# A hybrid attention layer on one core: attention phases, output weight splits and transposes moved, last block stored in three pieces

## The chip, the cores and the metric

One core of a Trainium2 chip runs the whole program. The time is the device time of one execution in microseconds (us), as the median of several executions; lower is better. Engines are named as the profile names them: PE (TensorE, matrix products), PEld (its weight loads), DVE (VectorE), ACT (ScalarE), POOL (GpSimd), SP (SyncE, which issues most transfers). Each engine runs its own instructions strictly in the order of the program and waits for the others by semaphores.

## The reference

The input x is 512 rows of 1024 numbers, float32. One layer is computed and a final normalisation follows:

```python
h = rmsnorm(x, norm_g)
p = h @ w_in                 # split into 14 column groups
y_gla  = rmsnorm(gated_linear_attention(gq, gk, gv, glog)) * silu(ggate)      # 4 heads, 384 columns
y_dsa  = dsa_mixer(dq, dk, dv, q_idx, k_idx, w_idx, rel_bias) * silu(dgate)   # 6 heads, 384 columns
y_pool = (windowed means of pu, minus pu) @ pool_w * pool_scale * silu(pgate) # 256 columns
x = x + concat(y_gla, y_dsa, y_pool) @ w_out
out = rmsnorm(x) * final_norm_g
```

dsa_mixer is causal softmax attention in which each row attends to the 128 visible keys with the highest indexer score (exactly the top 128), with a relative position bias.

## The kernel before, in words

**Tiles.** The 512 rows are 4 blocks of 128 (i or t = 0 to 3). Matrix products are made float32-exact out of three products of "high" and "low" parts: a tile is rounded to its high part by ACT (`hi_of`, L96), the rest becomes the low part on DVE (`lo_of`, L99), and PE computes high by high, low by high and high by low.

**First stage: input projections.** w_in comes in chunks of columns. A chunk's two halves (512 input rows each) are loaded by SP (`load_next`, L888), split by `half`, and multiplied by `proj_n` (one block of rows per step, L187) or `proj_t` (transposed, 128 columns per step, L199). A step of `proj_t` is 2 x 12 products of 512 columns into one PSUM bank. The order of the chunks that matter here is n4, dg, pg, c2, c1, pu, c0; c2, c1 and c0 hold the queries and keys of head pairs g = 2, 1, 0, pu and pg are the pooling branch, dg the attention gate.

**What sets the order.** The table `after` (L637 to L678) is written by hand: its key (chunk, step, "mid") names what is issued between the two halves of a projection step, (chunk, step) what is issued after the step, and "end" what is issued after its result has been taken out of PSUM. Everything hung in there is issued in that order on every engine that it uses. The top-k selection (`topk`, DVE, L458 and L459) fills the first stage in small portions.

**Linear attention (GLA).** For each block t: `gla_scores`, `gla_out` (PE L527, L531), `gla_norm`, `gla_gated` (DVE L564 writes gg), and `gla_turn`: PE transposes gg into the bank tpg (L571), ACT makes yGh, DVE yGl.

**Attention phases.** For block i and head pair g, named as letter, block, pair ("q02" is att_q(0, 2)): l lays the bias and mask into L on POOL (L689 to L696); q makes the scores on PE (L708), adds and takes the minimum on DVE (L710), and the exponential on ACT (L712); n takes the reciprocal of the sums on DVE (L719) and scales on POOL (L721); t transposes on PE (L730) and copies, the first head by ACT, the second by DVE (L732); v multiplies with the values (L741), DVE gates (yt, L744), ACT makes yDh; y makes yDl on DVE. The queries and keys of a pair are moved to the partitions where the scores need them by transfers that SP issues, QQ (L376) for the queries, KK and KL (L382) for the keys.

**Output weights.** w_out comes in four chunks wo0 to wo3. `out_high(n, h)` (ACT, tile oh) and `out_low(n, h)` (DVE, tile ol) split quarter h of chunk n, two instructions of 128 x 512 each. The first pieces of output weights take the tiles with the tags wh and wl, of which there are four each (bufs=4); the chunks before them in these four are pu half 0, pu half 1, c0 half 0 and c0 half 1, so out_high(0, 0) takes the tile of wh_pu0 and out_low(0, 0) that of wl_pu0.

**Second stage, `finish` (L815 on).** `out_part(t, a, e, kinds)` (PE L772) adds the products of block t for columns a to e of the output for G (GLA, 9 products), P (pooling, 6) and D (attention, 9); between these calls stand the remaining phases of pairs 1 and 0, the pooling products (`pool_mix`, PE L595, DVE L596), yPl (`pool_low`) and the splits. `residual` adds x, `out_norm` and `out_close` normalise and store. `out_last` (L793) does so for the last block, whose second half of columns comes in two pieces, 512 to 768 and 768 to 1024, so that only the last 256 columns stand behind the last matrix product:

```python
E = T + 256                                  # T = 512, D = 1024
out_part(t, E, D, "GPD", first=True, last=True)
```

Of the kernel before, what the change touches and what calls it, by code (L numbers as in the profile page):

```python
# [13 lines left out]
AF = mybir.ActivationFunctionType  # L14
ALU = mybir.AluOpType
# [3 lines left out]
T = 512  # L19
# [50 lines left out]
def hybrid_layer(  # L70
# [547 lines left out]
    def phase(n):  # L618
# [31 lines left out]
        ("dg", 0): [partial(gla_norm, 1), partial(gla_turn, 0), *halves("pg1"), partial(topk, 1, 1)],  # L650
        ("dg", 1, "mid"): [partial(gla_out, 2), partial(gla_scores, 3), partial(gla_gated, 1)],
        ("dg", 1): [partial(gla_norm, 2), partial(gla_turn, 1), *halves("c20", "c21"), partial(topk, 1, 3)],
        ("pg", 0, "mid"): [partial(gla_out, 3), partial(gla_gated, 2), partial(topk, 1, 2, 3)],
        ("pg", 0): [partial(gla_norm, 3), partial(gla_turn, 2), *halves("c10"), partial(topk, 1, 3)],
        ("pg", 1, "mid"): [partial(gla_gated, 3), partial(topk, 1, 2, 3)],
# [8 lines left out]
        ("c1", 0, "end"): [*halves("c00"), partial(topk, 1, 2)],  # L664
        ("c1", 1, "mid"): [partial(topk, 1, 2, 3)],
        ("c1", 1): [lambda: nc.gpsimd.memset(up[:, :, 0:16], 0.0), *att("l02", "l12"), partial(topk, 1, 3)],
        ("c1", 1, "end"): [lambda: load_next(), *halves("c01"), partial(topk, 16, 2, 3), *att("q02")],
        ("pu", 0, "mid"): att("n02", "q12"),
        ("pu", 0): att("t02", "n12", "l22"),
        ("pu", 1, "mid"): att("v02", "t12", "l32", "q22"),  # L670
        ("pu", 1): [*att("n22", "y02", "v12"), lambda: out_high(0, 0), lambda: pool_branch(0)],
        ("c0", 0, "mid"): [lambda: out_low(0, 0), *att("t22", "q32", "y12")],
        ("c0", 0): att("n32", "l01"),
        ("c0", 0, "end"): [lambda: out_high(1, 0), lambda: load_next(), *att("v22"), lambda: pool_branch(1)],
        ("c0", 1, "mid"): [lambda: out_low(1, 0), *att("t32", "q01", "l11", "y22")],
        ("c0", 1): att("n01"),
        ("c0", 1, "end"): [*att("v32", "q11", "l21"), lambda: out_high(0, 1)],
# [115 lines left out]
    def out_last(t):  # L793
        ts_ = slice(t * P, (t + 1) * P)
        E = T + 256
# [14 lines left out]
        nc.scalar.activation(xf[:, 0:T], xf[:, 0:T], AF.Copy, scale=fs[:, 4:5])  # L810
        nc.scalar.dma_start(o2[ts_, 0:T], xf[:, 0:T])
        nc.vector.tensor_scalar(xf[:, T:D], xf[:, T:D], fs[:, 4:5], None, op0=ALU.mult)
        nc.sync.dma_start(o2[ts_, T:D], xf[:, T:D])

    def finish():  # L815
# [7 lines left out]
        do("n11", "t01", "q21", "l00", "y32")  # L823
        out_high(1, 1)
        out_part(1, 0, T, "G", first=True)
        do("n21", "v01", "t11")
        out_low(1, 1)
        do("q00", "l31")
# [5 lines left out]
        pool_mix()  # L834
        out_part(2, 0, T, "G", first=True)
        do("n00", "v11", "t21", "y01")
        pool_low()
        do("q31", "l10")
        out_part(0, 0, T, "P")
        out_low(2, 0)  # L840
        do("n31", "v21", "t00", "q10", "l20", "y11")
        out_high(3, 0)
        out_part(1, 0, T, "P")
        do("n10", "v00", "t31", "q20", "l30", "y21")
        out_low(3, 0)
        out_high(2, 1)
        do("y00")
        out_part(2, 0, T, "P")
        out_part(0, 0, T, "D", last=True)
        do("n20", "v31", "t10", "q30")  # L850
        out_low(2, 1)
        out_high(3, 1)
        residual(0, 0, T, 0)
        out_low(3, 1)
# [25 lines left out]
        out_part(3, T, T + 256, "GPD", first=True, last=True)  # L880
# [7 lines left out]
    def load_next():  # L888
        n = len(chunks)
        if n < len(plan):  # L890
            chunks.append(load_chunk(*plan[n][:2]))
# [11 lines left out]
    def out_high(n, h):  # L903
        part, j = divmod(n, 2)
        cs = slice(256 * j, 256 * j + 256)
        for q in (2 * h, 2 * h + 1):
            if j == 0:
                WO[part].append(out_tiles(part, q))
            hi_of(WO[part][q][0][:, :, cs], chunks[n_in + n].raw[q // 2][:, 2 * (q % 2):2 * (q % 2) + 2, 0:256])
# [216 lines left out]
```

## Time and profile before

| what | value |
|---|---|
| median of 3 executions | 262.05 us (261.85 to 262.07) |
| profiled execution | 262.02 us, span in the profile 260.2 us |
| granted clock over it | 0.994 |
| PE busy | 245.0 us, 94% |
| DVE busy | 197.4 us, 76% |
| ACT, POOL busy | 119.6 us and 103.3 us |

The span runs from the first to the last instruction that the profile shows; 1.8 us lie around it. Times of the trace count from the start of the span. "Busy" of PE counts matrix products that overlap one another in the pipeline, so the time that one product really takes is read from start to start, not from its own length.

### The profile page before, as it was taken

What the parts mean: (1) busy time and instruction counts of PE and PEld (TensorE: products, weight loads), DVE (VectorE), ACT (ScalarE), POOL (GpSimd) and SP (SyncE); (2) the same over time, 40 slices, a digit from 0 to 9 for tenths busy, and PEclk for the clock granted to TensorE, in tenths of its full rate; (3) what the DMA queues carried; (4) which work ended last, traced back from release to release, by engine and by line L of the source; (5) the groups of instructions that cost most, each with busy time, mean ns of one, the idle gap of its engine ahead of it and who ended that gap; (6) DMA issues with size and microseconds to landing.
All of it is one profiled execution on the core that took longest, in us unless ns stands there. A gap on an engine that the chain in (4) does not pass through costs nothing.

```text
span 260.2 us, 4199 instructions
## 1 busy us (share of the span) xinstructions
PE 245.0 (94%) x1498; PEld 203.8 (78%) x1498; DVE 197.4 (76%) x442; ACT 119.6 (46%) x251; POOL 103.3 (40%) x109
## 2 busy tenths in 40 slices
PE   8999999999999999899999989998989978999990
PEld 4778889999999998688888867776756755788890
DVE  3999388899999999998999853599875877345322
ACT  5965186884836722225323353434465745222111
POOL 1645356354058630418534063618456562000011
PEclk9999999999999999999999999999999999999997
DMA  6994413225202150222314867605486000025012
GB/s 229 393 410 174 128 46 97 79 78 214 81 1 89 74 165 0 81 82 81 90 74 115 195 136 174 273 0 131 141 217 239 4 0 0 3 98 215 35 58 81
DMA packets 11780, 31.09 MB, mean 119 GB/s; under 512 B 1600, under 2 KB 1600, under 8 KB 11760
## 3 DMA queue, kind: packets, MB, share of 16 engines
q1 hardware_dynamic: 11328, 30.05, 36.2%
q10 hardware_dynamic: 432, 0.79, 0.9%
q8 instruction: 12, 0.20, 0.3%
q14 instruction: 8, 0.07, 0.1%
HBM read 23.91 MB, written 2.10 MB: 100 GB/s over the span
## 4 chain that ended last, share of the span: by engine, by line
PE 47%; DVE 36%; issue 6%; ACT 4%; DMA 3%; POOL 2%; SPq 1%; POOLq 0%; ACTq 0%; DVEq 0%
PE op L772 11%; DVE scs L459 8%; DVE m L458 6%; PE pf L973 5%; DVE ol L99 3%; PE pt_c L210 2%; PE pt_c L208 2%; PE pt_c L209 2%; DVE pm L583 2%; PE ov L741 2%; DMA wk<-in_w_in 2%; PE tpp L730 2%; ACT L L712 2%; DVE wl_n L99 2%; DVE wlk L99 2%
## 5 line engine op out<-in xcount | busy, mean ns | idle before, releaser
L721 POOL TENSOR_SCALAR L<-L,ast 128x128 f32<-128x128 f32 (+3 forms) x24 | 14.8, 630 | 34.1 <-DVE ast L719 34.1
L458 DVE MAX8 m<-scs 128x8 f32<-128x256 f32 (+2 forms) x48 | 26.5, 552 | 0.1
L459 DVE MATCH_REPLACE8 scs<-m,scs 128x256 f32<-128x256 f32 (+2 forms) x48 | 26.1, 543 | 0.0
L196 PE MATMUL pn_n<-wh_n,hTh 128*128 128x270 f32 (+1 forms) x128 | 21.6, 291 | 0.0
L196 PE MATMUL pn_n<-wl_n,hTh 128*128 128x270 f32 (+1 forms) x128 | 21.1, 287 | 0.0
L196 PE MATMUL pn_n<-wh_n,hTl 128*128 128x270 f32 (+1 forms) x128 | 21.0, 286 | 0.0
L712 ACT ACTIVATE L<-L,ast 128x128 f32<-128x128 f32 (+3 forms) x24 | 13.3, 557 | 16.0 <-DVE ast L710 15.1
L208 PE MATMUL pt_c<-hTh,wh_c 128*128 128x512 f32 x48 | 19.3, 402 | 0.0
L210 PE MATMUL pt_c<-hTh,wl_c 128*128 128x512 f32 x48 | 19.0, 395 | 0.0
L209 PE MATMUL pt_c<-hTl,wh_c 128*128 128x512 f32 x48 | 18.9, 394 | 0.0
L196 PEld LDWEIGHTS pn_n<-wh_n,hTh 128*128 128x128 f32 x128 | 18.2, 189 | 0.7 <-issue 0.4
L196 PEld LDWEIGHTS pn_n<-wl_n,hTh 128*128 128x128 f32 x128 | 18.0, 189 | 0.0
L196 PEld LDWEIGHTS pn_n<-wh_n,hTl 128*128 128x128 f32 x128 | 18.0, 189 | 0.0
L99 POOL TENSOR_TENSOR wl_c<-wr_c,wh_c 128x1024 fp32r<-128x1024 f32 x5 | 11.9, 2399 | 12.5 <-ACT wh_c L96 8.2
L967 POOL TENSOR_TENSOR acc<-acc,sqk 128x512 f32<-128x512 f32 x7 | 10.3, 1475 | 11.2 <-ACT sqk L965 11.2
L96 ACT ACTIVATE yDh<-yt 128x128 fp32r<-128x128 f32 x12 | 3.7, 310 | 21.8 <-DVE yt L744 21.8
L744 DVE TENSOR_TENSOR yt<-ov,dg 128x128 f32<-128x128 f32 x12 | 3.4, 285 | 13.2 <-PE ov L741 13.2
L99 POOL TENSOR_TENSOR wl_n<-wr_n,wh_n 128x1080 fp32r<-128x1080 f32 (+1 forms) x4 | 10.1, 2536 | 7.1 <-ACT wh_n L96 5.1
L689 POOL TENSOR_TENSOR L<-scs,TB 128x512 f32<-128x512 f32 x9 | 12.9, 1436 | 0.0
L778 ACT ACTIVATE sqo<-xr 128x512 f32<-128x512 f32 (+1 forms) x8 | 4.8, 604 | 16.9 <-DVE xr L777 10.6
L558 POOL TENSOR_TENSOR gss<-gss,hneg 128x4 f32<-128x4 f32 x4 | 4.1, 1014 | 21.4 <-DVE gss L557 21.4
L99 DVE TENSOR_TENSOR ol<-wr_wo,oh 128x512 fp32r<-128x512 f32 x16 | 11.2, 744 | 1.3 <-ACT oh L96 1.3
(241 smaller groups left out, 711.1 us busy)
## 6 DMA issues: line engine op xcount, KB each, us to landing
wr_wo<-in_w_out SPq DMA_DIRECT2D x8, 512.0 KB, 4.5
wr_c<-in_w_in SPq DMA_DIRECT2D x6, 512.0 KB, 3.9
wr_n<-in_w_in SPq DMA_DIRECT2D x4, 540.0 KB, 7.8
wr_n<-in_w_in SPq DMA_DIRECT2D x4, 536.0 KB, 3.5
xr<-in_x SPq DMA_DIRECT2D x4, 512.0 KB, 6.3
xk<-in_x_t SPq DMA_DIRECT2D x7, 256.0 KB, 5.5
wk<-in_w_in SPq DMA_DIRECT2D x6, 256.0 KB, 5.4
KK<-qkh SPq DMA_DIRECT2D x12, 128.0 KB, 2.5
```

The costliest lines, as they stand in the source:

```text
L99: return (eng or nc.vector).tensor_tensor(dst, src, hi.bitcast(F32), op=ALU.subtract)
L196: mm(ps[:, 0:n], a[:, k, ts_], w[:, k, :], start=(h + part + k == 0), stop=(h == 1 and part == 2 and k == 3))
L208: mm(ps[:, t0:T], c.hi[h][:, k, cs], hTh[h][:, k, t0:T], start=(h + k == 0), stop=False)
L209: mm(ps[:, t0:T], c.hi[h][:, k, cs], hTl[h][:, k, t0:T], start=False, stop=False)
L210: mm(ps[:, t0:T], c.lo[h][:, k, cs], hTh[h][:, k, t0:T], start=False, stop=(h == 1 and k == 3))
L458: nc.vector.max(out=m8, in_=msk[i])
L459: nc.vector.match_replace(out=msk[i], in_to_replace=m8, in_values=msk[i], imm_value=TAKEN)
L689: nc.gpsimd.tensor_tensor(L[:, :, near], msk[i][:, near].unsqueeze(1).to_broadcast([P, 2, 256]), TB[:, 2 * g:2 * g + 2, :], op=ALU.subtract)
L712: nc.scalar.activation(L[:, b, 0:n], L[:, b, 0:n], AF.Exp, bias=st[:, b:b + 1], scale=-1.0, accum_out=st[:, 2 + b:3 + b])
L721: nc.gpsimd.tensor_scalar(L[:, b, 0:n], L[:, b, 0:n], st[:, 4 + b:5 + b], 1.0, op0=ALU.mult, op1=ALU.mult)
L772: mm(outs[t][a][:, 0:e - a], lhs, rhs, start=(first and yi == 0 and rhs is wh and lhs is yh), stop=(last and yi == len(ys) - 1 and lhs is yl))
L973: mm(pns[t], a[:, t * P:(t + 1) * P], w, start=(k + part == 0), stop=(k == KT - 1 and part == 2))
```

## The change

The change moves hooks and calls and alters the last block's pieces. In the first stage `gla_turn(0)` to `gla_turn(2)` come half a step or more later, wo0 is loaded half a chunk earlier, q02 moves into the middle of the first pu step, `out_high(0, 0)` and `out_low(0, 0)` come right behind it, `out_high(1, 0)` and `out_low(1, 0)` follow at the next places, most phases of pair 2 move one place later, and q01 moves behind the whole second step of c0. In `finish`, the phases, splits and `pool_mix` are put in another order. The last block's second half is cut into 384 and 128 columns instead of 256 and 256, and its store is made in three pieces (ACT 0 to 384, SP 384 to 704 and 704 to 1024) instead of two halves.

```diff
-        ("dg", 0): [partial(gla_norm, 1), partial(gla_turn, 0), *halves("pg1"), partial(topk, 1, 1)],
-        ("dg", 1, "mid"): [partial(gla_out, 2), partial(gla_scores, 3), partial(gla_gated, 1)],
-        ("dg", 1): [partial(gla_norm, 2), partial(gla_turn, 1), *halves("c20", "c21"), partial(topk, 1, 3)],
-        ("pg", 0, "mid"): [partial(gla_out, 3), partial(gla_gated, 2), partial(topk, 1, 2, 3)],
-        ("pg", 0): [partial(gla_norm, 3), partial(gla_turn, 2), *halves("c10"), partial(topk, 1, 3)],
-        ("pg", 1, "mid"): [partial(gla_gated, 3), partial(topk, 1, 2, 3)],
+        ("dg", 0): [partial(gla_norm, 1), *halves("pg1"), partial(topk, 1, 1)],
+        ("dg", 1, "mid"): [partial(gla_out, 2), partial(gla_turn, 0), partial(gla_scores, 3), partial(gla_gated, 1)],
+        ("dg", 1): [partial(gla_norm, 2), *halves("c20", "c21"), partial(topk, 1, 3)],
+        ("pg", 0, "mid"): [partial(gla_out, 3), partial(gla_turn, 1), partial(gla_gated, 2), partial(topk, 1, 2, 3)],
+        ("pg", 0): [partial(gla_norm, 3), *halves("c10"), partial(topk, 1, 3)],
+        ("pg", 1, "mid"): [partial(gla_turn, 2), partial(gla_gated, 3), partial(topk, 1, 2, 3)],
...
-        ("c1", 0, "end"): [*halves("c00"), partial(topk, 1, 2)],
+        ("c1", 0, "end"): [lambda: load_next(), *halves("c00"), partial(topk, 1, 2)],
...
-        ("c1", 1, "end"): [lambda: load_next(), *halves("c01"), partial(topk, 16, 2, 3), *att("q02")],
-        ("pu", 0, "mid"): att("n02", "q12"),
-        ("pu", 0): att("t02", "n12", "l22"),
-        ("pu", 1, "mid"): att("v02", "t12", "l32", "q22"),
-        ("pu", 1): [*att("n22", "y02", "v12"), lambda: out_high(0, 0), lambda: pool_branch(0)],
-        ("c0", 0, "mid"): [lambda: out_low(0, 0), *att("t22", "q32", "y12")],
-        ("c0", 0): att("n32", "l01"),
-        ("c0", 0, "end"): [lambda: out_high(1, 0), lambda: load_next(), *att("v22"), lambda: pool_branch(1)],
-        ("c0", 1, "mid"): [lambda: out_low(1, 0), *att("t32", "q01", "l11", "y22")],
-        ("c0", 1): att("n01"),
-        ("c0", 1, "end"): [*att("v32", "q11", "l21"), lambda: out_high(0, 1)],
+        ("c1", 1, "end"): [*halves("c01"), partial(topk, 16, 2, 3)],
+        ("pu", 0, "mid"): [*att("q02"), lambda: out_high(0, 0)],
+        ("pu", 0): [lambda: out_low(0, 0), *att("n02", "q12")],
+        ("pu", 1, "mid"): [*att("t02", "n12", "l22"), lambda: out_high(1, 0)],
+        ("pu", 1): [*att("v02", "t12", "l32", "q22"), lambda: out_low(1, 0), lambda: pool_branch(0)],
+        ("c0", 0, "mid"): att("n22", "y02", "v12", "q32"),
+        ("c0", 0): att("t22", "n32", "l01"),
+        ("c0", 0, "end"): [lambda: load_next(), *att("y12")],
+        ("c0", 1, "mid"): [*att("v22", "t32", "l11"), lambda: pool_branch(1)],
+        ("c0", 1): att("q01"),
+        ("c0", 1, "end"): [*att("y22", "v32", "l21"), lambda: out_high(0, 1)],
...
-        E = T + 256
+        E = T + 384
...
-        nc.scalar.activation(xf[:, 0:T], xf[:, 0:T], AF.Copy, scale=fs[:, 4:5])
-        nc.scalar.dma_start(o2[ts_, 0:T], xf[:, 0:T])
-        nc.vector.tensor_scalar(xf[:, T:D], xf[:, T:D], fs[:, 4:5], None, op0=ALU.mult)
-        nc.sync.dma_start(o2[ts_, T:D], xf[:, T:D])
+        nc.scalar.activation(xf[:, 0:384], xf[:, 0:384], AF.Copy, scale=fs[:, 4:5])
+        nc.scalar.dma_start(o2[ts_, 0:384], xf[:, 0:384])
+        for a, e in ((384, 704), (704, D)):
+            nc.vector.tensor_scalar(xf[:, a:e], xf[:, a:e], fs[:, 4:5], None, op0=ALU.mult)
+            nc.sync.dma_start(o2[ts_, a:e], xf[:, a:e])
...
-        do("n11", "t01", "q21", "l00", "y32")
+        do("n01", "q11", "l00", "y32")
...
-        do("n21", "v01", "t11")
+        pool_mix()
+        do("t01", "n11", "q21", "l31")
         out_low(1, 1)
-        do("q00", "l31")
...
-        pool_mix()
         out_part(2, 0, T, "G", first=True)
-        do("n00", "v11", "t21", "y01")
+        do("v01", "t11", "n21", "q00", "l10")
         pool_low()
-        do("q31", "l10")
         out_part(0, 0, T, "P")
+        do("y01", "v11", "t21", "n00", "q31", "l20")
         out_low(2, 0)
-        do("n31", "v21", "t00", "q10", "l20", "y11")
         out_high(3, 0)
         out_part(1, 0, T, "P")
-        do("n10", "v00", "t31", "q20", "l30", "y21")
+        do("y11", "v21", "t00", "n31", "q10", "l30")
         out_low(3, 0)
         out_high(2, 1)
-        do("y00")
         out_part(2, 0, T, "P")
-        out_part(0, 0, T, "D", last=True)
-        do("n20", "v31", "t10", "q30")
+        do("v00", "y21", "t31", "y00", "n10", "q20")
         out_low(2, 1)
         out_high(3, 1)
+        out_part(0, 0, T, "D", last=True)
+        do("v31", "t10", "n20", "q30")
+        out_low(3, 1)
         residual(0, 0, T, 0)
-        out_low(3, 1)
         out_part(0, T, D, "GP", first=True)
...
-        out_part(3, T, T + 256, "GPD", first=True, last=True)
+        out_part(3, T, T + 384, "GPD", first=True, last=True)
```

Three places of the program show how the instructions now stand. The first is ACT's order at the end of c1 and in pu, before the change (wh_c_1781 is the high part of c0's second half; ast is the small tile of minima and sums, oh the high part of the output weights):

```order
L96 ACTIVATE wh_c_1781<-wr_c_1578 128x1024
L712 ACT_TABLE_LOAD
L712 ACTIVATE L_1764,ast_1785<-L_1764,ast_1785 128x128 x2
L712 ACTIVATE L_1766,ast_1816<-L_1766,ast_1816 128x256 x2
L732 COPY pt_1842<-tpp_1840 128x128
L96 ACTIVATE yDh<-yt_1870 128x128
L732 COPY pt_1876<-tpp_1873 128x256
```

The same stretch of ACT with the change:

```order
L96 ACTIVATE wh_c_1781<-wr_c_1578 128x1024
L712 ACT_TABLE_LOAD
L712 ACTIVATE L_1768,ast_1802<-L_1768,ast_1802 128x128 x2
L96 ACTIVATE oh_1813<-wr_wo_1729 128x2x256
L96 ACTIVATE oh_1816<-wr_wo_1729 128x2x256
L712 ACTIVATE L_1770,ast_1837<-L_1770,ast_1837 128x256 x2
L732 COPY pt_1863<-tpp_1861 128x128
```

The two oh instructions of out_high(0, 0) now stand between the exponentials of block 0 and of block 1 of pair 2.

The second place is DVE in pu, before the change (up is the pooling input that is taken out of pu's PSUM bank, pt the copies of the transposes):

```order
L719 RECIPROCAL ast_1785<-ast_1785 128x2
L710 ISA L_1766,ast_1816<-ps_1817,L_1766 128x256
L710 ISA ast_1816 128x1
L710 ISA L_1766,ast_1816<-ps_1818,L_1766 128x256
L710 ISA ast_1816 128x1
L388 TENSOR_TENSOR up<-pt_pu_1800,rsb 128x512
L732 COPY pt_1846<-tpp_1844 128x128
```

And with the change:

```order
L388 TENSOR_TENSOR up<-pt_pu_1789,rsb 128x512
L99 TENSOR_TENSOR ol_1814<-wr_wo_1729,oh_1813 128x2x256
L99 TENSOR_TENSOR ol_1817<-wr_wo_1729,oh_1816 128x2x256
L719 RECIPROCAL ast_1802<-ast_1802 128x2
L710 ISA L_1770,ast_1837<-ps_1838,L_1770 128x256
L710 ISA ast_1837 128x1
L710 ISA L_1770,ast_1837<-ps_1839,L_1770 128x256
```

The reciprocal of n02 now stands behind both ol instructions of out_low(0, 0); before, it stood ahead of pu's first `up`.

The third place is DVE in `finish`, around the split of chunk 3's first quarter (ol_2206) and the yDl of block 0, before the change:

```order
L710 ISA ast_2355 128x1
L99 TENSOR_TENSOR yDl<-yt_2298,yDh 128x128
L99 TENSOR_TENSOR ol_2206<-wr_wo_2209,oh_2205 128x2x256 x2
L99 TENSOR_TENSOR yDl<-yt_2338,yDh 128x128
L719 RECIPROCAL ast_2355<-ast_2355 128x2
```

And with the change, where ol_2184 is that split:

```order
L99 TENSOR_TENSOR ol_2184<-wr_wo_2187,oh_2183 128x2x256 x2
L744 TENSOR_TENSOR yt_2352<-ov_2349,dg 128x128
L99 TENSOR_TENSOR yDl<-yt_2307,yDh 128x128
L732 COPY pt_2368<-tpp_2363 128x512
L99 TENSOR_TENSOR yDl<-yt_2352,yDh 128x128
L719 RECIPROCAL ast_2321<-ast_2321 128x2
```

In both, the second yDl of the piece is block 0's of pair 0; it still follows the split, but PE's D products of block 0 now come later, behind out_low(2, 1) and out_high(3, 1).

## Rows read from the trace of the kernel before

**Rows 1.** The page: busy time, share of the span and instructions of each engine.

```profile
PE 245.0 (94%) x1498; PEld 203.8 (78%) x1498; DVE 197.4 (76%) x442; ACT 119.6 (46%) x251; POOL 103.3 (40%) x109
```

**Rows 2.** Windows: stretch, its length, busy of PE, PEld, DVE, ACT, POOL, clock, DMA.

```profile
152.00:186.00 34.00, 31.92 (x180) 25.19 (x180) 25.24 (x57) 13.84 (x36) 15.34 (x18) 1.00 0.49 144
186.00:221.00 35.00, 30.90 (x173) 21.87 (x171) 25.43 (x70) 20.49 (x57) 19.55 (x26) 1.00 0.30 91
```

**Rows 3.** PE's waits: line waited for, us in all, times, longest us.

```profile
PE ps L708 <- DMA QQ<-qkl: 2.1, 3, 0.9
PE op L772 <- DVE yDl L99: 1.5, 1, 1.5
PE tpg L571 <- DVE gg L564: 1.2, 1, 1.2
PE pp L595 <- DVE ast L710: 0.9, 1, 0.9
PE op L772 <- DVE ol L99: 0.5, 1, 0.5
PE op L772 <- DVE ast L710: 0.4, 1, 0.4
PE pp L595 <- DVE yt L744: 0.4, 1, 0.4
...
PE op L772 <- ACT oh L96: 0.3, 1, 0.3
```

**Rows 4.** Timeline of PE around gla_turn(0): start, length, idle before and its releaser.

```profile
105.45 0.40 PE L210 MATMUL pt_dg<-hTh,wl_dg 128*128 128x512 f32 x1
107.05 0.69 PE L571 MATMUL tpg<-ident,gg 128*128 128x128 f32 x3 [1.20 <-DVE gg L564]
```

**Rows 5.** Timeline of PE at q02.

```profile
153.20 0.30 PE L708 MATMUL ps<-KK,QQ 128*128 128x128 f32 x1 [0.83 <-DMA QQ<-qkl]
```

**Rows 6.** Timeline of pu: n02 on POOL, then two products of step 1's first half.

```profile
157.45 0.72 POOL L721 TENSOR_SCALAR L<-L,ast 128x128 f32<-128x128 f32 x2 [3.11 <-DVE ast L719]
...
160.04 0.40 PE L209 MATMUL pt_pu<-hTl,wh_pu 128*128 128x512 f32 x1
160.27 0.39 PE L210 MATMUL pt_pu<-hTh,wl_pu 128*128 128x512 f32 x1
```

**Rows 7.** The splits oh and ol: shortest, median and longest ns, first and last start.

```profile
L96 ACT ACTIVATE oh<-wr_wo x16: 615/617/619, 168.6 to 217.9; 128x512 fp32r<-128x512 f32 x16
L99 DVE TENSOR_TENSOR ol<-wr_wo,oh x16: 677/686/1530, 172.3 to 218.9; 128x512 fp32r<-128x512 f32 x16
```

**Rows 8.** Timeline of c0: the second pair of scans on DVE.

```profile
177.89 2.79 DVE L583 TENSOR_TENSOR_SCAN pm<-up 64x512 f32<-64x512 f32 x2
```

**Rows 9.** Timeline of PE in `finish`: the longest wait.

```profile
212.50 0.50 PE L772 MATMUL op<-oh,yDl 128*128 128x512 f32 x1 [1.46 <-DVE yDl L99]
```

**Rows 10.** Timeline of PE: products of 384 and of 128 columns, start to start.

```profile
192.43 0.28 PE L708 MATMUL ps<-KL,QQ 128*128 128x128 f32 x1
192.54 0.27 PE L708 MATMUL ps<-KK,QQ 128*128 128x128 f32 x1
...
207.29 0.34 PE L708 MATMUL ps<-KK,QQ 128*128 128x384 f32 x1
207.46 0.34 PE L708 MATMUL ps<-KL,QQ 128*128 128x384 f32 x1
```

**Rows 11.** Timeline of the end, from the last products to the stores.

```profile
253.64 0.28 PE L772 MATMUL op<-ol,yDh 128*128 128x256 f32 x1
253.75 0.28 PE L772 MATMUL op<-oh,yDl 128*128 128x256 f32 x1
254.07 0.42 DVE L804 TENSOR_TENSOR xr<-op,xr 128x256 f32<-128x256 f32 x1 [1.29 <-PE op L772]
...
255.93 0.72 ACT L810 ACTIVATE xf<-xf,fs 128x512 f32<-128x512 f32 x1 [3.73 <-POOL fs L808]
...
256.45 0.33 SPq L813 DMA_DIRECT2D out_y<-xf  x1
```

## The prediction

> **What bounds the kernel now.** I read the page first: PE is busy for 245.0 of 260.2 us, DVE 197.4, ACT and POOL less than half [rows 1]. So the time is PE's work plus its stops, and an instruction elsewhere counts only where PE waits for it. PE's waits, the second view, name the stops [rows 3]: 2.1 us in three for the queries' transfer QQ, 1.2 for gg, and six in the second stage, 0.9 + 0.4 + 1.5 + 0.4 + 0.3 + 0.5 = 4.0. Third, the windows [rows 2]: in 152 to 186 DVE is busy for 25.2 of 34 us and in 186 to 221 for 25.4 of 35, so no engine but PE is full, yet DVE, strictly in order, has stretches with no slack. The granted clock there is 1.00, the 2.4 GHz level, and nothing in the change touches it. Last, the timeline, for lengths. A stop costs more between starts than its idle time: from 105.45 to 107.05 are 1.60 us [rows 4], of which one product takes 0.23 (the spacing of [rows 6]), so 1.37 for 1.20 shown, some 0.15 more per stop.
>
> **The change, part by part** (plus is time gained).
>
> *gla_turn(0) to (2), later.* The stop before tpg goes: 1.4 us at most. In return the next GLA products wait for DVE's masked copies, which now have no stop in front of them, and tpg1 sits behind more of DVE's queue, where top-k keeps DVE full. Bounds 0 and +1.4; I take **+1.0**, nearer the row.
>
> *q02 half a step later.* It stands behind 12 more products, 12 x 0.23 = 2.8 us [rows 6]; the stop is 0.83 plus restart [rows 5]. PE comes 1.0 earlier from the first term, so QQ has 1.8 us to spare: **+1.0**, bounds +0.7 and +1.1. Loading wo0 earlier puts two issues on SP's queue ahead of the keys of pair 0. I cost it at nothing: those keys are wanted only at q00, deep in the second stage. Were that cover gone, it would be two issues of 0.33 [rows 11].
>
> *out_high(0, 0) and out_low(0, 0), the new wait.* They now stand right behind q02, but their tiles are those of wh_pu0 and wl_pu0, which PE reads until the end of pu step 1's first half. ACT's first oh stands there until that half is done; behind it in ACT's queue are the exponentials of L12 and the copy for t02. DVE's ol wait for oh, and behind them is the reciprocal of n02, as the second order piece shows. POOL's n02 waits for that, and PE's t02 comes right behind that very half, with nothing between. So PE stops for: first and second oh 0.62 + 0.62, the second ol 0.69 (the first runs beside the second oh) [rows 7], the reciprocal (about 0.2), half of n02's 0.72, 0.36 [rows 6], together 2.5, and the restart, 0.15 [rows 4]. **-2.7.** Bounds: -3.5 if ol takes the 1.53 of its longest row, and 0 if the tile is not held. Nothing can hide it, for every later PE instruction is behind t02. Result so far +1.0 + 1.0 - 2.7 = -0.7.
>
> *c0.* In front of the reciprocal of n22 DVE now has out_low(1, 0), 2 x 0.69, and pool_branch(0), whose two scans take up to 2.79 [rows 8]; with the reciprocal 4.3, and POOL's scaling of 384 columns by two, at most three times 0.72 [rows 6], 2.2: 6.5 in all. PE's work between q22 and t22 is two halves, 5.6, and v12 and q32, about 1: a tie. I take **-0.25**, bounds 0 and -1.2 (the scans have small instructions behind them, about 1 us). q01 goes behind the whole second step, so its two stops, 2.1 - 0.83 = 1.27 idle [rows 3, 5], go: with the restarts **+1.45**, bounds +1.2 and +1.6. At the start of the second stage that makes +0.5.
>
> *The second stage.* The six stops of 4.0 us cost 4.0 + 6 x 0.15 = 4.9. The new order takes their causes apart: the longest, 1.46 at 212.50 [rows 9], had two ol and two yDl between yt and the D products; now six calls, q20 and two more splits lie between, and yDl is no longer last. But DVE has the same work there. New stops that I find: pool_mix comes two calls earlier, so the second score of q21 and the third G wait for DVE's two gatings of pp, about 0.75; P of block 0 wants yPl, behind two ol and two maxima on DVE, about 1.0; out_low(3, 1) stands two calls in front of its reader, about 0.35. Together 2.1, so **+2.8**. Bounds: 0 (DVE's queue keeps the sum of the waits) and +4.9.
>
> *The last block.* Its second half was 24 + 24 products of 256 columns, 0.11 to 0.12 apart [rows 11]: 48 x 0.117 = 5.6. Now it is 24 of 384 columns, 0.17 to 0.18 apart [rows 10], and 24 of 128. Products of 128 columns come 0.11 to 0.13 apart [rows 10], no faster than those of 256, because each brings its own weights. 24 x 0.175 + 24 x 0.12 = 7.1: 1.5 lost. In the chain behind the last product, two DVE instructions shrink from 256 columns, 0.42 [rows 11], to 128: between 0 and 0.21 each, I take 0.14; ACT's scaling shrinks from 512 columns, 0.72, to 384: 0.12, at most 0.18; and ACT's store is a quarter smaller, about 0.1. SP has a second store to issue, 0.33 [rows 11], which ends about with ACT's. So 0.5 comes back: **-1.0**, bounds -1.5 and 0.
>
> The Trainium skill (page "TensorE: Matmul & The Clock Gate", section "Back-to-back issue gap") gives about 81 ns for a sustained weight load with a product of 128 columns. By it the last 24 would take 1.9 us, and the term would be about 0. This trace contradicts it so far: [rows 10] show 0.11, though for four products in a row only.
>
> Sum: 0.5 + 2.8 - 1.0 = +2.3. Against the profiled execution's 262.02: **259.7 us**; the median, 262.05, is the same within 0.03.
>
> **The rivals.**
>
> *The tile is not held long* (chance 0.19). If the weights' tiles were free when out_high(0, 0) comes, or POOL's n02 were early anyway, the -2.7 goes: 257.0. For it: ACT and DVE have slack in this stretch (DVE 25.2 of 34 [rows 2]). Against it: both order pieces and four tiles with four users in between.
>
> *Fast products of 128 columns* (0.08). If 24 in a row keep a shorter distance than four do, it is at least 0.059, half of the 256-column 0.117 [rows 11]; with 0.09, the middle between that and 0.12, the last block costs 24 x 0.03 = 0.7 less: 259.0. Against it: the row of 128 columns, where a shorter product came no sooner [rows 10]. The rule of the page above is this rival's.
>
> *Slower: DVE becomes the bound* (0.16). One mechanism: after the new wait DVE, having stood still for the held tile for about 3 us, starts pu's second step with its work undone. Place: n22 and then n32 in c0, behind pool_branch(0) and (1). Price: the full -1.2 there instead of -0.25, and the second stage begins with that queue, so its waits only change their names and the 2.8 is not earned: 259.7 + 0.95 + 2.8 = 263.4. It decides once DVE's 50.6 us of work between 152 and 221 [rows 2], the 3 us of standing still and its own waits for PE fill the 69 us, so from 15 us of such waits on. For it: the six stops of [rows 3] were DVE's in five cases. Against it: about a quarter of those 69 us is slack.
>
> *Nothing* (0.07). The second stage earns only 0.5, as new waits take the old ones' place: 262.0. That the change does nothing that it says is excluded by the order pieces.
>
> **How the numbers follow.** Forecast 0.50, tile not held 0.19, fast products 0.08, nothing 0.07, slower 0.16. Of this kernel a measurement can tell about 0.2%, 0.5 us, from no change. Faster by over 0.2% is 0.50 + 0.19 + 0.08 = 0.77, within it 0.07, slower 0.16. The forecast's own terms lie mostly within 1.3 of it, 258.4 to 261.0. For 8 in 10 the range goes down to 257.0, which leaves out half of the first rival's 0.19, and up to 262.8, which takes in "nothing" and leaves out two thirds of the slower case, about 0.1.
>
> **What the changed profile would show.** No wait of tpg for gg, none for QQ at q02 and q01. One wait of PE at the transposes of t02 behind pu step 1's first half, of 2.4 to 2.9 us, released by POOL's n02, with ACT's oh and DVE's ol standing idle before until PE's product: if it is absent the first rival holds. In the second stage the yDl stop gone and the sum of idle time near 2, not 4. In the last block products of 128 columns 0.11 to 0.13 apart; 0.09 or less would be the second rival. DVE's idle share in 186 to 221 near zero, with PE waiting 4 us or more, would be the slower rival. The forecast is wrong if t02's stop is under 1 or over 4 us, or the second stage's stops sum to over 4.

## The result and the profile after

The changed kernel took 263.84 us (four executions, 263.03 to 264.36), before 262.07: a ratio of 1.0062 with a 95% interval of 1.0049 to 1.0074. The forecast was 259.7, its range ended at 262.8, and the kernel became slower. A fifth execution, the profiled one, is left out, because PE ran at half speed throughout (485.5 us, products of 512 columns 0.45 us apart instead of 0.23), so the profile below is that of the same kernel run once more (*again* in the table of the experiments), 263.65 us with a span of 261.9.

The page, busy time, PE's slices and the granted clock [rows 1]:

```profile
PE 247.1 (94%) x1498; PEld 206.7 (79%) x1498; DVE 198.3 (76%) x443; ACT 119.0 (45%) x251; POOL 105.1 (40%) x109
...
PE   8999999999999999999999994699998989999991
...
PEclk9999999999999999999999999599999999999997
```

The work is that of before. New are the 4 and the 6 in PE's slices, and the 5 in the clock's: one stretch, between about 157 and 170 us. PE's waits, which answer to [rows 3]:

```profile
PE tpp L730 <- POOL L L721: 6.5, 2, 5.5
...
PE op L772 <- DVE yPl L99: 0.9, 1, 0.9
```

Every wait of [rows 3] that the prediction counted is gone: QQ, gg and the six of the second stage. In their place stand 0.9 for yPl and two at transposes, for POOL: one of 0.96 in the second stage (at 212.14) and one of 5.5 us at t02. The history of the long one in the timeline (start, length, idle before it and what ended that):

```profile
159.90 0.40 PE L210 MATMUL pt_pu<-hTh,wl_pu 128*128 128x512 f32 x1
160.10 1.15 ACT L96 ACTIVATE oh<-wr_wo 128x512 fp32r<-128x512 f32 x2 [3.40 <-PE pt_pu L209]
160.76 0.69 DVE L99 TENSOR_TENSOR ol<-wr_wo,oh 128x512 fp32r<-128x512 f32 x1 [2.98 <-ACT oh L96]
...
164.44 0.69 DVE L99 TENSOR_TENSOR ol<-wr_wo,oh 128x512 fp32r<-128x512 f32 x1 [2.99 <-DMA KL<-qkl]
165.05 0.16 DVE L719 RECIPROCAL ast<-ast 128x2 f32<-128x2 f32 x1
...
165.38 0.72 POOL L721 TENSOR_SCALAR L<-L,ast 128x128 f32<-128x128 f32 x2 [8.65 <-DVE ast L719]
...
165.81 0.82 PE L730 MATMUL tpp<-ident,L 128*128 128x128 f32 x2 [5.51 <-POOL L L721]
```

The chain is the forecast one, link by link: ACT's oh waits for PE's last product of the held tile, DVE's ol for oh, then the reciprocal, POOL, PE. But between the two ol stands a wait of 2.99 us for the transfer KL that the prediction does not have. And the products right behind the stop are slow:

```profile
166.28 0.78 PE L208 MATMUL pt_pu<-hTh,wh_pu 128*128 128x512 f32 x1
166.86 0.63 PE L209 MATMUL pt_pu<-hTl,wh_pu 128*128 128x512 f32 x1
167.28 0.63 PE L210 MATMUL pt_pu<-hTh,wl_pu 128*128 128x512 f32 x1
...
169.40 0.39 PE L209 MATMUL pt_pu<-hTl,wh_pu 128*128 128x512 f32 x1
169.63 0.40 PE L210 MATMUL pt_pu<-hTh,wl_pu 128*128 128x512 f32 x1
```

They start 0.43 us apart instead of 0.23, until about 169.4. The windows name the cause (stretch, its length, busy of PE, PEld, DVE, ACT, POOL, granted clock, DMA):

```profile
160.00:162.00 2.00, 0.30 (x2) 0.00 (x0) 0.69 (x1) 1.15 (x2) 0.00 (x0) 1.00 0.94 207
162.00:164.00 2.00, 0.00 (x0) 0.00 (x0) 0.00 (x0) 0.00 (x0) 0.00 (x0) 0.64 0.50 110
164.00:165.80 1.80, 0.00 (x0) 0.00 (x0) 1.35 (x5) 0.23 (x1) 0.42 (x2) 0.50 0.90 348
...
166.80:167.80 1.00, 1.00 (x4) 0.75 (x3) 0.23 (x2) 1.00 (x3) 0.67 (x2) 0.50 0.02 8
...
169.80:171.00 1.20, 1.20 (x8) 0.59 (x7) 0.24 (x1) 0.00 (x0) 1.20 (x2) 1.00 0.00 0
```

The granted clock was 1.00 (2.4 GHz) while PE worked, fell to 0.50 (1.2 GHz) while PE stood still, and stayed there for the first 3.6 us after it worked again. In that time seven products (166.28 to 169.40) lose 0.2 us each: 1.4.

Four landmarks show where the time went: the first product of c2, the first of the second stage, v10, and the last product. Before:

```profile
129.26 0.40 PE L208 MATMUL pt_c<-hTh,wh_c 128*128 128x512 f32 x1
186.23 0.39 PE L772 MATMUL op<-oh,yGh 128*128 128x512 f32 x1
220.95 0.66 PE L741 MATMUL ov<-pt,dv 128*64 128x128 f32 x8
```

with 253.75 for the last [rows 11], and after:

```profile
128.20 0.40 PE L208 MATMUL pt_c<-hTh,wh_c 128*128 128x512 f32 x1
189.10 0.50 PE L772 MATMUL op<-oh,yGh 128*128 128x512 f32 x1
221.73 0.66 PE L741 MATMUL ov<-pt,dv 128*64 128x128 f32 x8
255.78 0.28 PE L772 MATMUL op<-oh,yDl 128*128 128x128 f32 x1
```

So +1.06 to c2; -2.87 at the second stage, and -3.45 for equal work, as the four products of q11 (185.65 to 186.23 before) are now behind it; then +2.09, with q11 +2.67, up to v10; then -1.25 up to the last product. The span is 1.7 us longer than before, where the last product comes 2.0 later, so +0.3 comes back behind it.

### The profile page after: what moved, and what is told of

It is laid out like the page before. It is cut to its first block, busy times and chain, and to the rows that moved or that the text cites. A ratio compares the mean times of both kernels' runs of the same rounds, so it can differ in the third digit from the quotient of the medians.

```text
span 483.7 us, 4199 instructions
## 1 busy us (share of the span) xinstructions
PE 474.5 (98%) x1498; PEld 344.7 (71%) x1498; DVE 196.6 (41%) x443; ACT 122.0 (25%) x251; POOL 99.9 (21%) x109
## 4 chain that ended last, share of the span: by engine, by line
PE 95%; issue 3%; DVE 1%; POOL 0%; ACT 0%; POOLq 0%; DVEq 0%
PE pn_n L196 20%; PE op L772 16%; PE pf L972 9%; PE pt_c L208 5%; PE pt_c L209 5%; PE pt_c L210 5%; PE ov L741 3%; PE tpp L730 3%; PE ps L708 3%; PE pt_dg L208 2%; PE pt_pu L208 2%; PE pt_pu L209 2%; PE pt_pg L209 2%; PE pt_dg L209 2%; PE pt_pg L210 2%
## 5 line engine op out<-in xcount | busy, mean ns | idle before, releaser
L196 PE MATMUL pn_n<-wh_n,hTl 128*128 128x270 f32 (+1 forms) x128 | 38.1, 445 | 0.0
L196 PE MATMUL pn_n<-wh_n,hTh 128*128 128x270 f32 (+1 forms) x128 | 38.0, 464 | 0.0
L196 PE MATMUL pn_n<-wl_n,hTh 128*128 128x270 f32 (+1 forms) x128 | 37.8, 451 | 0.0
L196 PEld LDWEIGHTS pn_n<-wh_n,hTh 128*128 128x128 f32 x128 | 33.3, 309 | 1.8 <-issue 1.5
L196 PEld LDWEIGHTS pn_n<-wl_n,hTh 128*128 128x128 f32 x128 | 34.1, 331 | 0.0
L196 PEld LDWEIGHTS pn_n<-wh_n,hTl 128*128 128x128 f32 x128 | 33.5, 317 | 0.0
L210 PEld LDWEIGHTS pt_c<-hTh,wl_c 128*128 128x128 f32 x48 | 14.3, 297 | 8.3 <-issue 7.9
L208 PEld LDWEIGHTS pt_c<-hTh,wh_c 128*128 128x128 f32 x48 | 14.4, 300 | 7.5 <-issue 6.6
L730 PE MATMUL tpp<-ident,L 128*128 128x128 f32 x60 | 15.8, 433 | 2.2 <-POOL L L721 2.2
L772 PE MATMUL op<-oh,yGh 128*128 128x512 f32 (+2 forms) x27 | 17.1, 635 | 0.0
```

The costliest lines, as they stand in the source:

```text
L196: mm(ps[:, 0:n], a[:, k, ts_], w[:, k, :], start=(h + part + k == 0), stop=(h == 1 and part == 2 and k == 3))
L208: mm(ps[:, t0:T], c.hi[h][:, k, cs], hTh[h][:, k, t0:T], start=(h + k == 0), stop=False)
L210: mm(ps[:, t0:T], c.lo[h][:, k, cs], hTh[h][:, k, t0:T], start=False, stop=(h == 1 and k == 3))
L730: nc.tensor.transpose(tp[:, kb, :], L[:, b, kb * P:(kb + 1) * P], ident)
L772: mm(outs[t][a][:, 0:e - a], lhs, rhs, start=(first and yi == 0 and rhs is wh and lhs is yh), stop=(last and yi == len(ys) - 1 and lhs is yl))
```

## The experiments

All ran beside the kernel before (262.0 to 262.1 in each group).

| kernel | median us | ratio to before, 95% |
|---|---|---|
| again | 263.58 | 1.0059 [1.0036, 1.0081] |
| late_splits | 263.20 | 1.0038 [1.0020, 1.0056] |
| last_block | 262.72 | 1.0023 [1.0009, 1.0037] |
| moves_only | 262.48 | 1.0013 [1.0001, 1.0026] |
| half_split | 260.11 | 0.9926 [0.9907, 0.9945] |
| turns_only | 263.66 | 1.0046 [1.0028, 1.0064] |
| finish_only | 259.52 | 0.9909 [0.9894, 0.9923] |
| old_places | 263.93 | 1.0054 [1.0030, 1.0078] |
| half_256 | 258.57 | 0.9866 [0.9854, 0.9879] |
| no_hold | 258.86 | 0.9886 [0.9868, 0.9904] |
| no_turns | 260.25 | 0.9933 [0.9913, 0.9953] |
| half_load | 259.91 | 0.9916 [0.9896, 0.9936] |
| half_256_load | 259.96 | 0.9899 [0.9878, 0.9919] |

**again**: the changed kernel, unchanged.

> The changed kernel itself, once more, for a profile at full clock. Measured so far: 263.8 us, 4.1 over the forecast, at a mean granted clock of 0.981 to 0.986 where before had 0.994; (0.994 - 0.984) x 262 = 2.6 us of full clock are missing. Theory A (the stop costs the clock): PE stops for 2.4 to 2.9 us at the transposes of t02, and behind that stop the granted clock falls to its lower level for some us, so that the products right behind it come 0.46 instead of 0.23 us apart. Theory B (DVE is the bound): the lower clock lies elsewhere or costs nothing, DVE has no idle time between 186 and 221, and PE's stops there sum to 4 us or more. Theory C (last block): the part behind v10 is longer by 2 us or more.

The stop and the lower clock are there (above), the second stage's stops sum to 1.9 us (0.91 and 0.96), and the part behind v10 is 1.25 longer up to the last product: theory A, with a stop twice as long as it said.

**late_splits**: both splits of (0, 0) behind t02.

```diff
-("pu", 0, "mid"): [*att("q02"), lambda: out_high(0, 0)],
-("pu", 0): [lambda: out_low(0, 0), *att("n02", "q12")],
-("pu", 1, "mid"): [*att("t02", "n12", "l22"), lambda: out_high(1, 0)],
-("pu", 1): [..., lambda: out_low(1, 0), lambda: pool_branch(0)],
+("pu", 0, "mid"): att("q02"),
+("pu", 0): att("n02", "q12"),
+("pu", 1, "mid"): [*att("t02", "n12", "l22"), lambda: out_high(0, 0), lambda: out_high(1, 0)],
+("pu", 1): [..., lambda: out_low(0, 0), lambda: out_low(1, 0), lambda: pool_branch(0)],
```

> The change with out_high and out_low of (0, 0) placed behind t02, n12 and l22 (splits of (0, 0) and (1, 0) together there), so that their tiles are free when ACT and DVE come to them. Theory A: no stop at t02, no lower clock, 5 us less than the changed kernel: 2.7 for the stop and 2.6 for the clock, so 258 to 260 us. Theory B: the wait goes, but DVE has the same work in the second stage, so at most 2.7 less, 261 to 263 us, and the clock stays as it is. Theory C: no more than 1 us less.

The stop at t02 is gone, and the time is nearly the same. DVE now has four ol (3.47 us) and the scans in front of n22, so the stop has moved to t22:

```profile
175.12 1.41 PE L730 MATMUL tpp<-ident,L 128*128 128x128 f32 x6 [2.81 <-POOL L L721]
176.19 0.78 PE L208 MATMUL pt_c<-hTh,wh_c 128*128 128x512 f32 x1
176.76 0.63 PE L209 MATMUL pt_c<-hTl,wh_c 128*128 128x512 f32 x1
```

with the lower clock behind it again (in four of the twelve executions the mean granted clock was 0.991 or more, and these took 261.8 to 262.6 us), and one of 2.86 for DVE's `residual` follows in the second stage. So the tie that the prediction saw in front of n22 is real; two more ol tip it.

**last_block**: the last block's edit alone, on the kernel before.

> The kernel before with the last block's edit alone (384 and 128 columns, a store in three pieces). Forecast: 1.0 us longer than before, 263.1, with the 48 last products taking 7.1 instead of 5.6 us; if 24 products of 128 columns come 0.09 apart, 0.3 longer. Theory C: 2 us longer or more.

0.7 us longer. Products of 128 columns, 24 in a row, start 0.11 apart (254.75 and 254.86 are the last two). The tail behind them:

```profile
254.75 0.27 PE L772 MATMUL op<-ol,yDh 128*128 128x128 f32 x1
254.86 0.28 PE L772 MATMUL op<-oh,yDl 128*128 128x128 f32 x1
255.17 0.29 DVE L804 TENSOR_TENSOR xr<-op,xr 128x128 f32<-128x128 f32 x1 [0.71 <-PE op L772]
...
256.65 0.62 ACT L810 ACTIVATE xf<-xf,fs 128x384 f32<-128x384 f32 x1 [2.90 <-POOL fs L808]
```

DVE's addition fell from 0.42 to 0.29, ACT's scaling from 0.72 to 0.62: about what the prediction took.

**moves_only**: the change without the last block's edit.

> The change without the last block's edit (256 and 256 columns, a store in two halves). Theories A and B: 1.0 us less than the changed kernel, 262.8. Theory C: 2 us less or more, so 261.8 or below.

262.48, 1.1 below again. The last block explains 0.7 to 1.1 us of the loss and no more. Up to the last block this is the changed kernel, yet its profiled execution stopped for 4.60 us at t02, not 5.51:

```profile
164.87 0.82 PE L730 MATMUL tpp<-ident,L 128*128 128x128 f32 x2 [4.60 <-POOL L L721]
```

So the length of this stop differs between executions. Here SP issued the keys' transfers KL up to 160.0, in again up to 162.4.

**half_split**: only the first of the two pieces of the split (0, 0) stays early (`qs` chooses the pieces).

```diff
-("pu", 0, "mid"): [*att("q02"), lambda: out_high(0, 0)],
-("pu", 0): [lambda: out_low(0, 0), *att("n02", "q12")],
-("pu", 1, "mid"): [*att("t02", "n12", "l22"), lambda: out_high(1, 0)],
-("pu", 1): [..., lambda: out_low(1, 0), lambda: pool_branch(0)],
+("pu", 0, "mid"): [*att("q02"), lambda: out_high(0, 0, qs=(0,))],
+("pu", 0): [lambda: out_low(0, 0, qs=(0,)), *att("n02", "q12")],
+("pu", 1, "mid"): [*att("t02", "n12", "l22"), lambda: out_high(0, 0, qs=(1,)), lambda: out_high(1, 0)],
+("pu", 1): [..., lambda: out_low(0, 0, qs=(1,)), lambda: out_low(1, 0), lambda: pool_branch(0)],
```

> The change with only the first of the two pieces of out_high(0, 0) and out_low(0, 0) in front of n02; the second piece, whose low part waited for the transfer KL, stands behind t02, n12 and l22. Theory A1 (held tile plus KL): without KL the stop at t02 is the held tile's alone, 0.6 + 0.7 + 0.2 + 0.4 = 1.9 to 2.2 us instead of 5.5, and being so short it takes no clock behind it: 4.5 to 5.5 us less than the changed kernel at G of block 0, if the queue on DVE that stands in front of n22 then does not take it back as it did with both splits late (a stop of 2.8 us at t22 there). Theory A2 (the clock falls behind any stop here): a stop of about 2 and still products 0.43 us apart behind it. Theory B (DVE's queue): the stop moves to t22 whatever is done at t02, and G of block 0 starts later than 186.2, as in the kernel before.

260.1, 3.5 below again. The stop at t02 is 1.83 us, as long as the held tile alone makes it: the second piece and its wait for KL are what the other 3.7 us hung on. But of its six executions three took 259.3 to 259.6 with a mean granted clock of 0.991 to 0.993, and three 260.6 to 260.8 with 0.985 to 0.987: the clock fell in half of them, in the profiled one (260.65) behind that short stop.

**turns_only**: the three `gla_turn` alone, on the kernel before.

> The kernel before with the three moved gla_turn alone. The first c2 product started 1.06 us earlier with the change. If that is the gain of the transposes and the rest of the program keeps it: 1.0 less than before, 261.0. If PE's later waits (for QQ, then for DVE) take it back: 0 to 0.4 less.

Not less but 1.6 us more. c2 starts 0.97 earlier (128.29), but PE then stands before q02 for two transfers in a row (1.24 and 0.84, where before it stood 0.83 in all), and starts pu 0.4 later than before; PE's waits for QQ sum to 3.3 us instead of the 2.1 of [rows 3]. So the gain is taken back entirely at the old place of q02. In seven of twelve executions the clock fell (0.988 to 0.991, 263.6 to 264.2 us), in the profiled one of them behind these two stops; in the five others it was 0.994 to 0.997 and the time 262.1 to 262.5, so without the fall the turns alone gain nothing.

**finish_only**: the change's second stage alone, on the kernel before.

> The kernel before with the change's order of the second stage alone (n01 and q11 stay where they were, in the first stage). Forecast: 2.8 less than before, 259.2, with the stop at yDl gone. If DVE's work is the bound there: within 0.8 of before, 261.2 to 262.8, with other waits of about 4 us in all.

2.5 us less. PE's waits:

```profile
PE ps L708 <- DMA QQ<-qkl: 2.1, 3, 0.9
PE tpg L571 <- DVE gg L564: 1.2, 1, 1.2
...
PE op L772 <- DVE yPl L99: 1.0, 1, 1.0
PE tpp L730 <- POOL L L721: 1.0, 1, 1.0
```

The first stage's are as in [rows 3], the second stage's 4.0 us have become 2.0. This is by far the largest part of the change that pays.

**old_places**: all moves, but splits and load of wo0 beside the phases where they stood before (for the split (0, 0) that is half a step later), n22 ahead of the scans, last block as before.

> All moves of the change but the splits: out_high and out_low of (0, 0) and (1, 0) and the load of wo0 stay at the places of the kernel before, n22 comes ahead of pool_branch(0), and the last block is as before. If the splits' early place is what the change lost by: no stop at t02, clock whole, the gains of the transposes (1.0), q02 (1.0), q01 (1.4) and the second stage (2.8) in full would give 255.8; with half of them taken back by DVE's queue 258.9. If DVE is the bound from pu on, whatever the splits do: 261 or more.

The second stage starts at 182.72, 3.5 us earlier than before (2.9 for equal work, as q11 stands behind it here), and v10 comes at 220.99, no earlier. From 192 to 216 DVE is busy for 21.8 of 24 us, and of PE's stops in the second stage 5.5 us are for DVE, the longest for `residual`:

```profile
215.36 1.29 DVE L99 TENSOR_TENSOR ol<-wr_wo,oh 128x512 fp32r<-128x512 f32 x2
216.56 0.68 DVE L777 TENSOR_TENSOR xr<-op,xr 128x512 f32<-128x512 f32 x1
...
217.30 0.50 PE L772 MATMUL op<-oh,yGh 128*128 128x512 f32 x1 [2.86 <-DVE xr L777]
```

Here and in late_splits the products of block 0's second half get the PSUM bank that `residual` still reads; in finish_only the same products did not wait for it. Why the banks fell so was not followed up. The early start is lost at DVE. In six of ten executions the clock fell besides (263.9 to 264.9 us); the profiled one is of the other four (262.1 to 262.4).

**half_256**: half_split with the last block as before.

> The kernel of half_split with the last block as before (256 and 256 columns, a store in two halves): the new wait cut to the held tile, the price of the last block taken out. The last block alone cost 0.7 on the kernel before and 1.1 on the change, so 259.0 to 259.4 here against 260.1. If the clock's fall behind the stop of 1.8 us is by chance, its times come in two groups some 1.3 to 1.7 apart.

258.57, the best of all, 3.5 below before. Its stop at t02 is the same 1.83, and the clock held in all four executions (0.995 to 0.996):

```profile
162.03 0.68 PE L730 MATMUL tpp<-ident,L 128*128 128x128 f32 x2 [1.83 <-POOL L L721]
162.47 0.48 PE L208 MATMUL pt_pu<-hTh,wh_pu 128*128 128x512 f32 x1
162.78 0.40 PE L209 MATMUL pt_pu<-hTl,wh_pu 128*128 128x512 f32 x1
```

**no_hold**: nothing of the splits (0, 0) before t02, `residual(0)` right behind the D products.

```diff
-("pu", 0, "mid"): [*att("q02"), lambda: out_high(0, 0, qs=(0,))],
-("pu", 0): [lambda: out_low(0, 0, qs=(0,)), *att("n02", "q12")],
-("pu", 1, "mid"): [*att("t02", "n12", "l22"), lambda: out_high(0, 0, qs=(1,)), lambda: out_high(1, 0)],
-("pu", 1): [..., lambda: out_low(0, 0, qs=(1,)), lambda: out_low(1, 0), lambda: pool_branch(0)],
-("c0", 0, "mid"): att("n22", "y02", "v12", "q32"),
-("c0", 0): att("t22", "n32", "l01"),
+("pu", 0, "mid"): att("q02"),
+("pu", 0): att("n02", "q12"),
+("pu", 1, "mid"): [*att("t02", "n12", "l22"), lambda: out_high(0, 0)],
+("pu", 1): [..., lambda: out_low(0, 0)],
+("c0", 0, "mid"): [*att("n22", "y02", "v12"), lambda: out_high(1, 0), lambda: pool_branch(0), *att("q32")],
+("c0", 0): [lambda: out_low(1, 0), *att("t22", "n32", "l01")],
...
         out_part(0, 0, T, "D", last=True)
+        residual(0, 0, T, 0)
         do("v31", "t10", "n20", "q30")
         out_low(3, 1)
-        residual(0, 0, T, 0)
```

> As half_256, but nothing of the splits (0, 0) before t02: out_high and out_low (0, 0) stand behind it, (1, 0) one place later, n22 ahead of pool_branch(0), and residual(0) right behind the D products so that the next bank is free earlier. Theory A (the held tile and the clock are all that is lost): no stop at t02 and t22, 1.8 + up to 1.7 us less than half_256 at the start of the second stage, and 256 to 258 us in the end. Theory B (DVE is the bound from c0 on, once PE does not stop): the second stage starts earlier, but its stops grow by as much, and the time is within 1 us of half_256.

No stop at t02, but 1.49 at v22, for the copy of t22 on ACT, 0.47 at t32, and a second stage that starts at 184.60, against 184.22 in half_256. The time is within 0.3 of half_256: theory B. DVE is behind the first of these stops too: ACT's copy stands behind q32's exponentials, the first of which starts at 174.94, as soon as DVE, with two ol and the scans in front, has q32's first minimum done (174.86). The profiled execution took 259.83, 1.0 above the median, so the others may have shorter ones. Once the stop is down to 1.8 us, taking it away in this way gave nothing.

**no_turns**: half_256 with the three `gla_turn` at the old places.

> The kernel of half_256 with the three gla_turn at the places of the kernel before. On the kernel before the moved turns gained 1.06 us up to c2 and lost it again at q02, where the queries' transfer came no earlier. Here q02 stands 12 products later. If the gain of the turns is kept there: 1.0 more than half_256. If it only lengthens the wait for the held tile's transfers or DVE: within 0.4 of half_256.

With the clock whole 259.5 to 259.7, against 258.4 to 258.7: the 1.06 us are kept where q02 stands later. Three of six executions had the lower clock (260.8 to 261.1).

**half_load**: the change in full, but only the half of wo0 that the split (0, 0) reads is loaded early.

```diff
-("c1", 0, "end"): [lambda: load_next(), *halves("c00"), partial(topk, 1, 2)],
-("c1", 1, "end"): [*halves("c01"), partial(topk, 16, 2, 3)],
+("c1", 0, "end"): [lambda: load_next((0,)), *halves("c00"), partial(topk, 1, 2)],
+("c1", 1, "end"): [lambda: load_chunk("wo0", 256, (1,), chunks[-1]), *halves("c01"), partial(topk, 16, 2, 3)],
```

> The change with only the first half of wo0 (the half that out_high(0, 0) reads) loaded at the early place; the second half, which is wanted much later, is loaded behind KL as in the kernel before. In the change DVE's second ol waited for KL until 164.4, KL being issued up to 162.36 against 159.90 before. Theory A3 (the early load delays KL): KL is issued 1 to 2.5 us earlier, the stop at t02 shrinks from 5.5 to between 3 and 4.5 us, and the time by as much, to 261 to 262.5. Theory A4 (KL is late for another reason): stop and time within 0.5 of the change.

259.91, 3.7 below again, by moving one transfer: theory A3, with more gained than it said. SP's queue in again:

```profile
151.82 2.23 SPq L147 DMA_DIRECT2D wr_wo<-in_w_out  x2
154.15 4.62 SPq L382 DMA_DIRECT2D KK<-qkh  x4
158.85 3.51 SPq L382 DMA_DIRECT2D KL<-qkl  x4
```

and in half_load (whose lines stand one further down there):

```profile
151.67 0.59 SPq L148 DMA_DIRECT2D wr_wo<-in_w_out  x1
152.49 2.41 SPq L383 DMA_DIRECT2D KK<-qkh  x4
155.00 3.47 SPq L383 DMA_DIRECT2D KL<-qkl  x4
...
162.77 0.68 PE L731 MATMUL tpp<-ident,L 128*128 128x128 f32 x2 [2.43 <-POOL L L722]
```

KL is issued 3.9 us earlier, DVE's two ol run back to back, and the stop at t02 is 2.43 us. The order of SP's program with the waits on semaphores shows how one load does that in the change (the two loads of wo0, then KK and KL; DMAHW0 to 7 are the eight semaphores that transfers take in turn):

```
L147 DMA wr_wo_1729<-in_w_out 128x1024 [waits DMAHW7_49]
L147 DMA wr_wo_1731<-in_w_out 128x1024 [waits DMAHW0_49,Pool_49]
L382 DMA KK_112<-qkh_1763 64x512 [waits DMAHW1_49,Activation_49]
...
L382 DMA KL_119<-qkl_1764 64x512 [waits DMAHW7_49]
L382 DMA KL_119<-qkl_1764 64x512 [waits DMAHW0_49]
```

The second load waits for POOL, which still reads the tile that it overwrites (POOL's wl_c ends at 153.69, the load is issued at 153.72), and everything behind it on SP waits with it. The last KL takes the semaphore of that second load, and so waits for its 512 KB to land: the load landed 8.2 us after its issue, and this KL went out at 161.90. Of the 3.9 us by which the first KL is late, 1.7 are there at the first KK (154.15 against 152.49), the second load and its wait. The rest lies in the issues of KK: one of them took 2.79 us, where none in half_load took more than 0.60. What held it is not shown.

**half_256_load**: the same on half_256.

> The same split of wo0's load in the kernel of half_256, where nothing at t02 waits for KL. The stop there is the held tile's, 1.8 us, so the load has nothing to give: within 0.4 of half_256, 258.2 to 259.0. If POOL's table for block 2 or other readers of KL were late in half_256: up to 1 us less.

With the clock whole 258.5 and 258.7, as half_256: the load has nothing to give where nothing waits for KL. In the four other executions the clock fell (0.986 to 0.989, 259.9 to 260.2), in the profiled one of them behind the same stop of 1.83 us:

```profile
162.15 0.68 PE L731 MATMUL tpp<-ident,L 128*128 128x128 f32 x2 [1.83 <-POOL L L722]
...
163.41 0.63 PE L209 MATMUL pt_pu<-hTh,wh_pu 128*128 128x512 f32 x1
163.83 0.63 PE L210 MATMUL pt_pu<-hTl,wh_pu 128*128 128x512 f32 x1
164.26 0.63 PE L211 MATMUL pt_pu<-hTh,wl_pu 128*128 128x512 f32 x1
```

## Why the prediction was wrong

**The transposes**, +1.0: right, +1.06 measured, and no_turns shows that the gain lasts. **q02**, +1.0: right; no wait for QQ is left, and from the start of c2 to the last product before t02 the changed kernel is 1.16 faster for equal work.

**The stop at t02**, -2.7: the mechanism was right, its place and its chain too, and its size would have been right: 2.43 us in half_load, where all is as the sum had it. What failed is the sentence on the load of wo0: "I cost it at nothing: those keys are wanted only at q00." The keys' transfers have a second waiter. The text ahead of the prediction gives both pieces of the split the tiles wh and wl, but `out_tiles` (L893) gives these to the first piece only. The second has a tile of its own, and the program lays its low part over the tile qkl out of which KL is still being copied (both start at the same address). So DVE's second ol waits for KL to land, and behind it n02 and PE. And the price given in case that cover was gone, "two issues of 0.33", was wrong too: the second load waits for POOL and holds SP's queue, and the last KL waits for that load to land. In again KL went out 3.9 us later than with one load, and the stop became 5.51 instead of 2.43 (4.60 in moves_only). From start to start it cost 6.0 us (159.90 to 166.28, against 159.35 to 159.72 before), 3.3 more than forecast. The prediction's own sign of being wrong, a stop of over 4 us, had come.

**The clock**: "nothing in the change touches it" failed with it. The stop itself touched it: behind it the clock stayed at 0.50 for seven products, 1.4 us. Half_load shows the price once more: with a stop of 2.43 its executions took 259.2 to 259.3 at a granted clock of 0.992 to 0.993, or 260.5 to 260.7 at 0.986, 1.4 apart. In again no execution had more than 0.986.

Together that is 4.7. Up to the second stage the forecast had +0.5 and the trace has -3.45, so 3.95 were lost there; the transposes, q02 and c0 gave back the other 0.75. With the second half of the load out of the way, 259.7 lies between half_load's two groups.

**c0**: the tie before n22 fell on the good side, no stop (-0.25 taken; half_load has none there either), and q01's two stops went. What is left for c0 when the terms above are taken off the -3.45 is about +1.7, forecast +1.2. **The second stage**: +2.67 for +2.8, 2.5 in finish_only; the wait for yPl was 0.91 for an estimated 1.0, those at pp and of out_low(3, 1) did not come, one of 0.96 for POOL came instead. **The last block**: -0.95 (1.25 - 0.3) for -1.0, 0.7 alone. Products of 128 columns came 0.11 apart 24 times, so the second rival fell. The Trainium skill (page "TensorE: Matmul & The Clock Gate", section "Back-to-back issue gap") states about 81 ns for a sustained weight load with a product of 128 columns; the measurement, 0.11 us, decides against it here.

**The slower rival** gave 263.4, near the truth by luck, for a reason that is not the one of this kernel: DVE did not set the pace of the second stage in the change, whose stops there sum to 1.9 us. It is true of other kernels here. In old_places and, by way of ACT's copy, in no_hold, where PE does not stop in pu, DVE takes back what PE gains.

## What to carry to other kernels

Moving a load earlier on a queue is not free because its own data is wanted late: look for what stands behind it on that queue, what the load itself waits for, and every reader of the delayed transfers, also those that only wait for memory to be given back. An engine in order that is made to wait early passes the wait on to everything behind it; put such work behind the instruction that PE needs next, or split it so that only the free piece comes early (half_256: 258.57 us). Price a stop of PE with the slow products that can follow it.

## What was not expected of the hardware

Behind a short stop the same kernel's clock falls in some executions and not in others. By the mean granted clock of each execution it fell in 3 of 6 of half_split, in 3 of 6 of no_turns, in 4 of 6 of half_256_load and in none of 4 of half_256, all four with a stop of 1.83 us in their profile; in 3 of 6 of half_load (2.43), and in all 6 of again (5.51 in its profile). A fall cost 1.2 to 1.6 us, by the means of the two groups. In the kernel before, whose longest single stop in this part is 1.46 [rows 9], the mean granted clock was 0.992 or more in 67 of the 68 executions that ran beside the experiments; in the other it was 0.987, and the time 263.42 us, so a fall came there too, once. What decides between the two was not tried.

The Trainium skill (page "TensorE: Matmul & The Clock Gate", section "HAM oscillation — how this bites in real kernels") tells of a kernel whose waits for transfers put the clock back to its lower level again and again; the granted clock of 0.50 behind the stop of 5.51 us agrees. That it also falls behind 1.83 us, and then only at times, is what these runs add.
